# Hybrid decoder layer on one core: the recurrence without GpSimd arithmetic, with a shifted decay and v copied across halves

## The chip, the core and the metric

One core of a Trainium2 chip runs the whole layer. TensorE (PE) multiplies, with its weight loads shown apart as PEld; VectorE (DVE) and ScalarE (ACT) work element by element; GpSimd (POOL) does some arithmetic, memsets and DMA issue; SyncE (SP) issues the weight DMAs. The metric is the device time of one execution in microseconds; less is better. Each engine takes its instructions in the order in which the program has them.

## The reference

A decoder layer for 256 tokens of width 2048: RMSNorm, one input projection (6432 columns), then two groups side by side, 16 dilated-attention heads and 16 RWKV-7 heads, an output projection with residual, and a SwiGLU feed-forward of 5632 with residual and a last norm. The part around the change is the RWKV-7 group:

```python
decay = jnp.exp(-DECAY_SCALE * jax.nn.sigmoid(w0 + jnp.tanh(w_lo) @ w_up))
a = jax.nn.sigmoid(a0 + a_lo @ a_up)
kk = heads(k * k_k)
kk = kk / jnp.maximum(jnp.sqrt(jnp.sum(kk * kk, axis=-1, keepdims=True)), 1e-12)
k = k * (1.0 + (a - 1.0) * k_a)
xs = (rh, wh, kh, vh, -kk, kk * ah)          # by token
def rwkv7_step(state, inp):
    r, w, k, v, a, bb = inp
    sa = jnp.einsum('bhij,bhj->bhi', state, a)
    state = (state * w[:, :, None, :] + sa[..., None] * bb[:, :, None, :]
             + v[..., None] * k[:, :, None, :])
    y = jnp.einsum('bhij,bhj->bhi', state, r)
    return state, y
```

## The kernel before

All large products run in fp32r pieces: a weight tile `wr` that SP loads is split by ACT into `wh` (L148) and by DVE into the rest `wl` (L149, one 128x512 instruction), and PE multiplies three times (for the projections in transposed form L191 to L193, 128x256 each; for v and the later products L178 to L180). So every half weight tile costs DVE one L149, and twelve projection matmuls eat it up. PE's main stream of projections goes through the kernel from end to end.

The recurrence and the attention are side threads: Python generators whose steps are mixed into the main stream by a virtual clock (`run`, `step`; a `yield 2.0` asks for a pause of so much), so the order on each engine is fixed when the program is built. The RWKV heads come in two halves of 8 heads (`half` 0 and 1). A half works on tiles of 4 x 256 columns (4 pairs of heads, 256 tokens) in these stages:

- `keys` (L513 on): `tha` is the tanh of the a gate, `kp` the changed key, `kn` the key at unit length, with `blocksum` for sums over 64 rows;
- `core`: `thp` and its scan `sc` (L552) are the logarithm of the decay, summed over 64 tokens; `pw` (L557) and `ipw` (L559) are the decay from the chunk's start and its inverse, inclusive of the token, `pm` (L561) the exclusive one; `ar` holds per chunk of 64 tokens the key side (index 0, L572) and the receptance side (index 1, L586); `bk` holds the products with `ipw` (L580, L582);
- 64x64 products `Ah` (L616), and the inverse of a triangular matrix by 31 steps on DVE (`T1`, L655 and L657, from `nu`, which a DMA brings); `T1` and its transpose go to DRAM (L673, L676) and come back by quarters as `T` and `U64` (L688, L689, issued on ACT's queue) for the products `C0` and `C1`; then the chunk loop (`Xh`, `Yh`, `Zh`, `Hh`);
- `end`: two `blocksum` of y (L783), two of its squares `sq` (L787), the gate product `gh` (16 matmuls, L796) and the last factors (L789 to L800). The `end` of half 0 stands amid the `core` of half 1.

`blocksum` (L478 on) cuts a tile into halves of 512 columns; for each, ACT writes `bh` (L483), DVE the rest `bl` (L484), and PE adds L487 (with `bh`) and L488 (with `bl`) in its order. v is put into a tile `vs` with the two 64-token halves exchanged (L596, GpSimd), transposed on PE (L640) and copied by ACT (L642) into `vv`.

Of the kernel before, what the change touches and what calls it, by code (L numbers as in the profile page):

```python
# [10 lines left out]
F32 = mybir.dt.float32  # L11
F32R = mybir.dt.float32r
AF = mybir.ActivationFunctionType
ALU = mybir.AluOpType
AX = mybir.AxisListType

P = 128
SEQ = 256
D = 2048
HD = 64  # L20
# [10 lines left out]
DS = math.exp(-0.5)  # L31
# [44 lines left out]
def layer(ctx: ExitStack, tc: tile.TileContext, I, out, dbg=None, upto=99):  # L76
# [344 lines left out]
    for dst, c0, n, i in ((wa, 0, 128, 0), (gl0, 128, 128, 1), (gl1, 256, 32, 2)):  # L421
        pt = opsum(f"ptlo{i}")
# [38 lines left out]
    def rwkv_side(half, hb, H, e, Z):  # L461
# [46 lines left out]
        def ln_table(ins):  # L508

            with tc.issue_after(getattr(ins, "ins", ins)):  # L510
                ACT.preload_act_table_set("natural_log_exp_and_others")

        def keys():  # L513

            tha = e(7, "tha") if half == 0 else e(3, "tha")
            yield from up(tha, lo_up()[64:128, :], wa[64:128, :], AF.Tanh, 8, "a")
            if half == 1:
                ln_table(Z["tanh"])
            zk = yield from need("zk")

            kp = e(8, "kp") if half == 0 else e(10, "kp")
            for hp in range(4):
                b = hb + hp
                DVE.tensor_scalar(kp[:, hp, :], tha[:, hp, :], hv[:, 16 + b:17 + b], hv[:, 24 + b:25 + b],
                                  op0=ALU.mult, op1=ALU.add)
            yield 2.0
            POOL.tensor_tensor(fl(kp), fl(kp), fl(zk), op=ALU.mult)

            kn = (e(9, "kn") if half == 0 else
                  act_p.tile([P, 4, SEQ], F32, tag="mx0", name=f"kn_{H}"))  # L530
            for hp in range(4):
                ACT.activation(kn[:, hp, :], zk[:, hp, :], AF.Square, scale=hpc(V_KK, hp))
            yield from blocksum(kn, lambda pt, sl: DVE.tensor_scalar(fl(kn)[:, sl], pt, 1e-24, None, op0=ALU.max))
            ACT.activation(fl(kn), fl(kn), AF.Ln)
            yield 2.0
            ACT.activation(fl(kn), fl(kn), AF.Exp, scale=-0.5)
            yield 2.0
            for hp in range(4):
                DVE.scalar_tensor_tensor(kn[:, hp, :], zk[:, hp, :], hpc(V_KK, hp), kn[:, hp, :],
                                         op0=ALU.mult, op1=ALU.mult)  # L540
            yield EL
            DVE.scalar_tensor_tensor(fl(tha), fl(tha), 1.0, fl(kn), op0=ALU.add, op1=ALU.mult)
            Z["tha"], Z["kp"], Z["kn"] = tha, kp, kn

        def core():
# [6 lines left out]
                DVE.tensor_tensor_scan(sc[:, hp, :], packc(C_SCAN, SEQ), thp[:, hp, :], 0.0,  # L552
                                       op0=ALU.mult, op1=ALU.add)
            yield 2.0
            POOL.tensor_tensor(fl(thp), fl(sc), fl(thp), op=ALU.subtract)
            pw = e(6, "pw")
            ACT.activation(fl(pw), fl(sc), AF.Exp, scale=-0.5 * DS)  # L557
            yield 2.0
            ACT.activation(fl(sc), fl(sc), AF.Exp, scale=0.5 * DS)  # L559
            yield 2.0  # L560
            ln_table(ACT.activation(fl(thp), fl(thp), AF.Exp, scale=-0.5 * DS))  # L561
            ipw, pm = sc, thp
            pcs = rp.tile([P, 4, 4], F32, tag="pcs", name=f"pcs{H}")
            DVE.tensor_copy(pcs, pw[:, :, HD - 1::HD])

# [3 lines left out]

            ar = rp.tile([P, 4, 4, 2, HD], F32, tag="ar", name=f"ar{H}")  # L570
            yield EL
            DVE.scalar_tensor_tensor(ar[:, :, :, 0, :], ch(kn), -1.0, ch(pm), op0=ALU.mult, op1=ALU.mult)  # L572
            yield EL

            bk = [e(i, f"bk{i}").rearrange("p a (c w t) -> p (a c) w t", w=2, t=HD) for i in (4, 2)]
# [1 line left out]
            for g in range(2):  # L577
                for c2 in range(2):
                    pr = lambda a: ch(a)[:, 2 * g:2 * g + 2, c2::2, :]
                    DVE.scalar_tensor_tensor(bk[g][:, :, c2::2, c2, :], pr(tha), 0.5, pr(ipw),  # L580
                                             op0=ALU.mult, op1=ALU.mult)
                    POOL.tensor_tensor(bk[g][:, :, c2::2, 1 - c2, :], pr(ipw), pr(kp), op=ALU.mult)  # L582
                yield EL

            zr = yield from need("zr")
            POOL.tensor_tensor(ar[:, :, :, 1, :], ch(zr), ch(pw), op=ALU.mult)  # L586
            yield EL
            for hp in range(4):
                DVE.scalar_tensor_tensor(kp[:, hp, :], zr[:, hp, :], hpc(V_RK, hp), kp[:, hp, :],
# [1 line left out]
            zv = yield from need("zv")  # L591
            yield from blocksum(kp, lambda pt, sl: DVE.tensor_tensor(fl(kp)[:, sl], pt, fl(zv)[:, sl], op=ALU.mult))
            bonus = kp
            vs = rp.tile([P, 4, 2, P], F32, tag="e9", name=f"vs{H}")
            for c2 in range(2):
                POOL.tensor_copy(vs[:, :, :, 64 * (1 - c2):64 * (1 - c2) + 64], ch(zv)[:, :, c2::2, :])  # L596

# [23 lines left out]
                    q = 2 * c2 + b  # L623
                    ACT.dma_start(block(d1, q)[:, 8 * cp:8 * cp + 8, :], abk[quarter(q), c, :, 32 * b:32 * b + 32])
            flat = lambda t: t.rearrange("p a b -> p (a b)")[0:HD].rearrange("p (s t) -> p s t", t=32)
            T1 = flat(e(3, "T1"))
            POOL.memset(T1, 0.0)
            POOL.memset(T1.rearrange("p a b -> p (a b)")[:, 0::33], 1.0)

            vv = [e(i, f"vv{i}").rearrange("p (c a) (b i) -> p c (a b) i", c=2, i=HD) for i in (5, 7)]  # L630
            for c in range(4):
# [5 lines left out]
            for cp in range(2):  # L637
                pt = opsum(f"tv{H}{cp}")
                for hp in range(4):
                    PE.transpose(pt[:, hp * P:(hp + 1) * P], vs[:, hp, cp], ident)  # L640
                for c2 in range(2):
                    ACT.copy(vv[cp][half_of(1 - c2), c2, :, :], pt[half_of(1 - c2)].rearrange("p (h j) -> p h j", j=HD))  # L642
                if cp == 0:
                    nu = flat(e(6, "nu"))
                    ACT.dma_start(nu, d1.rearrange("u (s t) -> u s t", t=32))
                yield
            yield LAT[0]


# [469 lines left out]
```

## Time and profile before

| | us |
|---|---|
| median of 3 runs | 1251.55 (1250.91 to 1253.92) |
| the profiled execution's own time | 1252.15 |
| its span, first to last instruction | 1250.2 |
| PE busy in the span | 1227.6 (98%) |
| DVE busy | 815.4 (65%) |
| ACT busy | 692.9 (55%) |
| POOL busy | 63.7 (5%) |

The span is what the views divide; the execution's own time has 1.95 us more around it. A busy PE in this table only says that some matmul was under way; time that it lost shows as idle time before an instruction, with the instruction that ended it, and as a granted clock below 1.

### The profile page before, as it was taken

The page shows a single profiled execution, that of the slowest core. Times are in us where ns is not written, and L with a number is a line of the kernel's source. Part 1 is how long each engine was busy: PE and PEld are TensorE (multiplying, and loading weights), DVE is VectorE, ACT ScalarE, POOL GpSimd, SP SyncE. Part 2 cuts the span into 40 slices and gives each one's busy share as a digit, 9 for nine tenths or more (in the row PEclk, how much of TensorE's full clock was granted, in tenths as well). Part 3 has the DMA queues.
Part 4 walks back from the last instruction along what each step waited for, and adds up shares of the span by engine and source line. Part 5 has one row for each costly group of instructions (what it writes and reads, how often), then busy time and mean ns, then how long its engine had stood idle before and what let it go on. Part 6 is the DMA issues. An engine that isn't in the chain of part 4 may idle for free.

```text
span 1250.2 us, 21170 instructions
## 1 busy us (share of the span) xinstructions
PE 1227.6 (98%) x7930; PEld 1065.7 (85%) x7930; DVE 815.4 (65%) x1519; ACT 692.9 (55%) x1312; POOL 63.7 (5%) x69
## 2 busy tenths in 40 slices
PE   7999999999999999999999999999999999999997
PEld 6999997888899788888888888888888888888885
DVE  5787885587946857665665666666566565555653
ACT  7755655555645756565555655555565554454443
POOL 3140000120000000000000000000000000010100
PEclk9999999999999999999999999999999999999999
DMA  8657575335563476666666666666666666666664
GB/s 236 185 151 199 153 193 139 111 113 135 157 178 106 145 226 215 180 186 190 187 191 194 187 188 193 192 187 186 197 189 187 191 193 187 195 188 193 183 201 134
DMA packets 147879, 223.24 MB, mean 179 GB/s; under 512 B 18123, under 2 KB 65489, under 8 KB 147649
## 3 DMA queue, kind: packets, MB, share of 16 engines
q1 hardware_dynamic: 132176, 211.12, 57.7%
q10 hardware_dynamic: 13920, 6.06, 2.0%
q0 software_dynamic: 1680, 4.72, 1.1%
q8 instruction: 62, 1.02, 0.3%
q14 instruction: 41, 0.33, 0.1%
HBM read 218.17 MB, written 3.69 MB: 177 GB/s over the span
## 4 chain that ended last, share of the span: by engine, by line
PE 90%; DVE 4%; DMA 3%; ACT 1%; issue 1%; SPq 0%; POOLq 0%; POOL 0%; ACTq 0%; DVEq 0%
PE up L1000 13%; PE gb L1000 7%; PE ga L1000 7%; PE up L1001 6%; PE d L178 6%; PE d L180 6%; PE d L179 6%; PE gb L1001 3%; PE ga L1001 3%; DMA wr<-in_w_in_dram 2%; PE o L179 2%; PE o L180 2%; PE o L178 2%; PE qTb L191 1%; PE zrh L191 1%; PE qTb L192 1%
## 5 line engine op out<-in xcount | busy, mean ns | idle before, releaser
L149 DVE TENSOR_TENSOR wl<-wr,wh 128x512 fp32r<-128x512 f32 (+1 forms) x792 | 549.6, 700 | 367.6 <-ACT wh L148 350.9
L148 ACT ACTIVATE wh<-wr 128x512 fp32r<-128x512 f32 (+1 forms) x792 | 492.1, 627 | 470.7 <-DVE wl L149 202.1
L1000 PE MATMUL up<-u,wh 128*128 128x512 f32 x704 | 244.6, 394 | 0.0
L1001 PE MATMUL up<-u,wl 128*128 128x256 f32 x704 | 195.0, 277 | 0.0
L1000 PEld LDWEIGHTS up<-u,wh 128*128 128x128 f32 x704 | 132.0, 188 | 30.6
L1001 PEld LDWEIGHTS up<-u,wl 128*128 128x128 f32 x704 | 132.2, 188 | 0.0
L178 PE MATMUL d<-wh,hh 128*128 128x512 f32 x336 | 131.5, 391 | 0.0
L179 PE MATMUL d<-wl,hh 128*128 128x512 f32 x336 | 131.5, 391 | 0.0
L180 PE MATMUL d<-wh,hl 128*128 128x512 f32 x336 | 131.5, 391 | 0.0
L1000 PE MATMUL gb<-u,wh 128*128 128x512 f32 x352 | 130.4, 394 | 0.0
L1000 PE MATMUL ga<-u,wh 128*128 128x512 f32 x352 | 130.1, 394 | 0.0
L1001 PE MATMUL gb<-u,wl 128*128 128x256 f32 x352 | 97.6, 277 | 0.0
L1001 PE MATMUL ga<-u,wl 128*128 128x256 f32 x352 | 97.6, 277 | 0.0
L1000 PEld LDWEIGHTS ga<-u,wh 128*128 128x128 f32 x352 | 66.0, 188 | 15.3
L1000 PEld LDWEIGHTS gb<-u,wh 128*128 128x128 f32 x352 | 66.0, 188 | 15.3
L180 PEld LDWEIGHTS d<-wh,hl 128*128 128x128 f32 x336 | 63.2, 188 | 13.8
L179 PEld LDWEIGHTS d<-wl,hh 128*128 128x128 f32 x336 | 63.2, 188 | 13.8
L178 PEld LDWEIGHTS d<-wh,hh 128*128 128x128 f32 x336 | 63.2, 188 | 13.8
L1001 PEld LDWEIGHTS gb<-u,wl 128*128 128x128 f32 x352 | 66.2, 188 | 0.0
L1001 PEld LDWEIGHTS ga<-u,wl 128*128 128x128 f32 x352 | 66.0, 188 | 0.1
L1053 POOL TENSOR_TENSOR h_sb<-h_sb,fg 128x512 f32<-128x512 f32 x6 | 9.9, 1659 | 663.0 <-ACT jd L1051 663.0
L191 PE MATMUL kTb<-u1h,wh 128*128 128x256 f32 x128 | 38.1, 298 | 0.0
(293 smaller groups left out, 2095.6 us busy)
## 6 DMA issues: line engine op xcount, KB each, us to landing
wr<-in_w_gate_up_dram SPq DMA_DIRECT2D x176, 512.0 KB, 4.3
wr<-in_w_in_dram SPq DMA_DIRECT2D x96, 512.0 KB, 3.8
wr<-in_w_down_dram SPq DMA_DIRECT2D x88, 512.0 KB, 4.5
wr<-in_w_out_dram SPq DMA_DIRECT2D x32, 512.0 KB, 4.7
wr<-in_w_in_dram SPq DMA_DIRECT2D x8, 288.0 KB, 6.1
x_sb<-in_x_dram SPq DMA_DIRECT2D x8, 256.0 KB, 6.6
biasa<-rvd ACTq DMA_DIRECT2D x4, 512.0 KB, 4.7
xs<-in_x_dram POOLq DMA_DIRECT2D x4, 512.0 KB, 6.4
```

What stands on the lines that cost most here:

```text
L148: ACT.activation(hi[:, :, :n], src, AF.Copy)
L149: DVE.tensor_tensor(lo[:, :, :n], src, hi[:, :, :n].bitcast(F32), op=ALU.subtract)
L178: PE.matmul(o, ah[:, sl], hi[:, :n], start=first, stop=False)
L179: PE.matmul(o, ah[:, sl], lo[:, :n], start=False, stop=False)
L180: PE.matmul(o, al[:, sl], hi[:, :n], start=False, stop=fin)
L191: PE.matmul(o, hi[:, cb], uh_, start=kc == 0, stop=False)
L192: PE.matmul(o, hi[:, cb], ul_, start=False, stop=False)
L1000: PE.matmul(ps[b], hi[:, cb], u, start=kc == 0, stop=False)
L1001: PE.matmul(ps[b][:, 0:SEQ], lo[:, cb], u[:, 0, :], start=False, stop=kc == NK - 1)
L1053: POOL.tensor_tensor(hs, hs, fg[:, cs], op=ALU.mult)
```

## The change

In words: five operations go from GpSimd to DVE, namely `kp` times `zk` (L527, one 128x1024 instruction in each half), the four products of `bk` (L582; in the new file L583) and `zr` times `pw` (L586, now four instructions, L588). The exclusive decay `pm` is not made any more: GpSimd's subtraction (L555) and ACT's third exponential (L561) go, and the key side of `ar` takes `pw` of the token before (four instructions of 63 columns, and one for each chunk's first token, where the exclusive decay is 1; L570 and L572 of the new file). The exchanged copy `vs` (L596) goes; v is transposed as it is, and ACT's copy moves the result across the two halves of the partitions. The two memsets of `T1` stay on GpSimd but stand behind the transposes of v.

```diff
             yield 2.0
-            POOL.tensor_tensor(fl(kp), fl(kp), fl(zk), op=ALU.mult)
+            DVE.tensor_tensor(fl(kp), fl(kp), fl(zk), op=ALU.mult)
...
-            POOL.tensor_tensor(fl(thp), fl(sc), fl(thp), op=ALU.subtract)
             pw = e(6, "pw")
             ACT.activation(fl(pw), fl(sc), AF.Exp, scale=-0.5 * DS)
             yield 2.0
-            ACT.activation(fl(sc), fl(sc), AF.Exp, scale=0.5 * DS)
-            yield 2.0
-            ln_table(ACT.activation(fl(thp), fl(thp), AF.Exp, scale=-0.5 * DS))
-            ipw, pm = sc, thp
+            ln_table(ACT.activation(fl(sc), fl(sc), AF.Exp, scale=0.5 * DS))
+            ipw = sc
...
-            DVE.scalar_tensor_tensor(ar[:, :, :, 0, :], ch(kn), -1.0, ch(pm), op0=ALU.mult, op1=ALU.mult)
+            DVE.tensor_scalar(ar[:, :, :, 0, 0:1], ch(kn)[:, :, :, 0:1], -1.0, None, op0=ALU.mult)
+            for hp in range(4):
+                DVE.scalar_tensor_tensor(ar[:, hp, :, 0, 1:HD], ch(kn)[:, hp, :, 1:HD], -1.0,
+                                         ch(pw)[:, hp, :, 0:HD - 1], op0=ALU.mult, op1=ALU.mult)
...
-                    POOL.tensor_tensor(bk[g][:, :, c2::2, 1 - c2, :], pr(ipw), pr(kp), op=ALU.mult)
+                    DVE.tensor_tensor(bk[g][:, :, c2::2, 1 - c2, :], pr(ipw), pr(kp), op=ALU.mult)
...
-            POOL.tensor_tensor(ar[:, :, :, 1, :], ch(zr), ch(pw), op=ALU.mult)
+            for hp in range(4):
+                DVE.tensor_tensor(ar[:, hp, :, 1, :], ch(zr)[:, hp], ch(pw)[:, hp], op=ALU.mult)
...
-            vs = rp.tile([P, 4, 2, P], F32, tag="e9", name=f"vs{H}")
-            for c2 in range(2):
-                POOL.tensor_copy(vs[:, :, :, 64 * (1 - c2):64 * (1 - c2) + 64], ch(zv)[:, :, c2::2, :])
...
-            T1 = flat(e(3, "T1"))
-            POOL.memset(T1, 0.0)
-            POOL.memset(T1.rearrange("p a b -> p (a b)")[:, 0::33], 1.0)
...
-                    PE.transpose(pt[:, hp * P:(hp + 1) * P], vs[:, hp, cp], ident)
+                    PE.transpose(pt[:, hp * P:(hp + 1) * P], zv[:, hp, cp * P:(cp + 1) * P], ident)
                 for c2 in range(2):
-                    ACT.copy(vv[cp][half_of(1 - c2), c2, :, :], pt[half_of(1 - c2)].rearrange("p (h j) -> p h j", j=HD))
+                    ACT.copy(vv[cp][half_of(1 - c2), c2, :, :], pt[half_of(c2)].rearrange("p (h j) -> p h j", j=HD))
...
+            T1 = flat(e(3, "T1"))
+            POOL.memset(T1, 0.0)
+            POOL.memset(T1.rearrange("p a b -> p (a b)")[:, 0::33], 1.0)
             yield LAT[0]
```

The pauses of the threads shift with it, and so does the order on each engine. Three places matter. The first is DVE where the `end` of half 0 and the `core` of half 1 meet, from the second `blh` of y (L484) to the first `blh` of its squares; before:

```order
L484 TENSOR_TENSOR blh0_3256<-y_h0_2801,bhh0_3255 128x512
L149 TENSOR_TENSOR wl71_0_3242<-wr71_3239,wh71_0_3241 128x512
L783 SCALAR_TENSOR_TENSOR y_h0_2801<-bsh0_3272,y_h0_2801 128x512
L149 TENSOR_TENSOR wl71_1_3246<-wr71_3239,wh71_1_3245 128x512
L564 COPY pcsh1_3278<-pw_h1_3227 128x16
L572 SCALAR_TENSOR_TENSOR arh1_3280<-kn_h1_2727,thp_h1_3151 128x16x64
L580 SCALAR_TENSOR_TENSOR bk4_h1_3326<-tha_h1_2633,sc_h1_3197 128x4x64 x2
L149 TENSOR_TENSOR wl72_0_3290<-wr72_3287,wh72_0_3289 128x512
L149 TENSOR_TENSOR wl72_1_3294<-wr72_3287,wh72_1_3293 128x512
L589 SCALAR_TENSOR_TENSOR kp_h1_2670<-zr_h1_1885,par_76,kp_h1_2670 128x256 x2
L149 TENSOR_TENSOR wl73_0_3341<-wr73_3338,wh73_0_3340 128x512
L484 TENSOR_TENSOR blh0_3306<-sq_h0_3303,bhh0_3305 128x512
```

The same stretch of DVE in the changed kernel:

```order
L484 TENSOR_TENSOR blh0_3257<-y_h0_2803,bhh0_3256 128x512
L149 TENSOR_TENSOR wl71_0_3243<-wr71_3240,wh71_0_3242 128x512
L561 COPY pcsh1_3262<-pw_h1_3228 128x16
L783 SCALAR_TENSOR_TENSOR y_h0_2803<-bsh0_3277,y_h0_2803 128x512
L149 TENSOR_TENSOR wl71_1_3247<-wr71_3240,wh71_1_3246 128x512
L572 SCALAR_TENSOR_TENSOR arh1_3264<-kn_h1_2729,pw_h1_3228 128x4x63 x4
L149 TENSOR_TENSOR wl72_0_3295<-wr72_3292,wh72_0_3294 128x512
L581 SCALAR_TENSOR_TENSOR bk4_h1_3314<-tha_h1_2635,sc_h1_3199 128x4x64
L583 TENSOR_TENSOR bk4_h1_3314<-sc_h1_3199,kp_h1_2672 128x4x64
L149 TENSOR_TENSOR wl72_1_3299<-wr72_3292,wh72_1_3298 128x512
L484 TENSOR_TENSOR blh0_3311<-sq_h0_3308,bhh0_3310 128x512
```

One weight piece (`wl73_0`) and two `kp` products now come behind the last row; one former GpSimd product (L583) and the `ar` in four pieces stand ahead of it. Between the two `blh` of `sq` DVE now has three 128x256 and 128x512 rows (L581, L583, `wl73_0`).

The second place is the next stretch of DVE in the changed kernel, from the second `blh` of `sq` to the first `blh` of half 1's `kp`:

```order
L484 TENSOR_TENSOR blh0_3363<-sq_h0_3308,bhh0_3362 128x512
L149 TENSOR_TENSOR wl73_1_3353<-wr73_3346,wh73_1_3352 128x512
L588 TENSOR_TENSOR arh1_3264<-zr_h1_1884,pw_h1_3228 128x4x64 x4
L591 SCALAR_TENSOR_TENSOR kp_h1_2672<-zr_h1_1884,par_76,kp_h1_2672 128x256 x2
L149 TENSOR_TENSOR wl74_0_3403<-wr74_3400,wh74_0_3402 128x512
L789 TENSOR_TENSOR y_h0_2803<-y_h0_2803,sq_h0_3308 128x1024
L484 TENSOR_TENSOR blh1_3391<-kp_h1_2672,bhh1_3390 128x512
```

Before, one `wl` alone stood between these two `blh`, and L789 behind them.

The third is PE at the second attention quad of the first head half: before, the products `AVh10` of half 1's recurrence came behind its transposes `PTa1`:

```order
L868 MATMUL PTa10_3989<-ident_72,sa1_3941 128x128 x2
L868 MATMUL PTa11_3995<-ident_72,sa1_3941 128x128 x3
L667 MATMUL AVh10_4001<-vv5_h1_3686,abkh1_3552 64x64 x16
L875 MATMUL Oa10_4019<-pTa10_3990,vb0_2986 64x256
L875 MATMUL Oa10_4019<-pTa11_3996,vb0_2986 64x256
```

In the changed kernel they stand right behind the scores `Sa1`:

```order
L842 MATMUL Sa110_3964<-kTb0_3459,qTb0_2991 128x256
L842 MATMUL Sa111_3965<-kTb0_3459,qTb0_2991 128x256
L667 MATMUL AVh10_3974<-vv5_h1_3661,abkh1_3534 64x64 x16
L179 MATMUL vb1_1_4066<-wl83_0_4076,u1h1_89 128x512
L180 MATMUL vb1_1_4066<-wh83_0_4075,u1l1_93 128x512
```

From `Sa1` to the first `PTa1` PE then has 25 matmuls of the main stream and the `AVh10`, where before it had 32 of the main stream. Elsewhere PE's order is nearly the old one; the second half's products come 12 projection matmuls earlier.

## Rows read from the trace of the kernel before

**Rows 1.** The page, busy time of each engine in us (share), number of instructions.

```profile
PE 1227.6 (98%) x7930; PEld 1065.7 (85%) x7930; DVE 815.4 (65%) x1519; ACT 692.9 (55%) x1312; POOL 63.7 (5%) x69
```

**Rows 2.** Waits of PE: line, who ended them, us in total, times, longest.

```profile
PE bsh L488 <- DVE blh L484: 5.0, 3, 2.8
```

**Rows 3.** Windows of 10 us: busy us of PE, PEld, DVE, ACT, POOL; clock, DMA.

```profile
80.00:90.00 10.00, 10.00 (x86) 10.00 (x85) 10.00 (x13) 4.47 (x8) 10.00 (x5) 1.00 0.61 172
...
250.00:260.00 10.00, 7.51 (x58) 7.14 (x58) 9.97 (x13) 6.86 (x10) 3.98 (x3) 1.00 0.24 60
260.00:270.00 10.00, 9.70 (x45) 7.68 (x46) 6.87 (x13) 4.62 (x7) 3.21 (x5) 0.83 0.43 133
```

**Rows 4.** Timeline of PE: start, us, instruction, count, [idle before, ended by].

```profile
112.97 0.51 PE L488 MATMUL bsh<-blh,onesblk 128*128 128x512 f32 x1 [0.65 <-DVE blh L484]
...
248.08 0.28 PE L192 MATMUL qTb<-u1l,wh 128*128 128x256 f32 x1
249.96 0.51 PE L488 MATMUL bsh<-blh,onesblk 128*128 128x512 f32 x1 [1.60 <-DVE blh L484]
...
257.11 0.28 PE L193 MATMUL qTb<-u1h,wl 128*128 128x256 f32 x1
257.23 0.28 PE L191 MATMUL qTb<-u1h,wh 128*128 128x256 f32 x1
260.30 0.50 PE L488 MATMUL bsh<-blh,onesblk 128*128 128x512 f32 x1 [2.79 <-DVE blh L484]
```

**Rows 5.** Timeline of DVE ahead of these waits.

```profile
111.26 1.05 DVE L149 TENSOR_TENSOR wl<-wr,wh 128x512 fp32r<-128x512 f32 x1
...
247.47 0.75 DVE L822 TENSOR_TENSOR qTb<-qTb,rbc 128x256 f32<-128x256 f32 x2
248.13 1.77 DVE L484 TENSOR_TENSOR blh<-y_h,bhh 128x512 fp32r<-128x512 f32 x1
249.82 2.89 DVE L149 TENSOR_TENSOR wl<-wr,wh 128x512 fp32r<-128x512 f32 x1
...
255.17 1.32 DVE L580 SCALAR_TENSOR_TENSOR bk_h<-tha_h,sc_h 128x256 f32<-128x256 f32 x2
256.41 1.83 DVE L149 TENSOR_TENSOR wl<-wr,wh 128x512 fp32r<-128x512 f32 x2
...
259.56 0.68 DVE L484 TENSOR_TENSOR blh<-sq_h,bhh 128x512 fp32r<-128x512 f32 x1
```

**Rows 6.** Timeline of POOL in the same stretch.

```profile
246.97 2.38 POOL L555 TENSOR_TENSOR thp_h<-sc_h,thp_h 128x1024 f32<-128x1024 f32 x1 [4.58 <-DVE sc_h L552]
249.31 2.85 POOL L586 TENSOR_TENSOR arh<-zr_h,pw_h 128x1024 f32<-128x1024 f32 x1
255.28 1.81 POOL L582 TENSOR_TENSOR bk_h<-sc_h,kp_h 128x256 f32<-128x256 f32 x2 [3.12 <-DVE arh L572]
```

**Rows 7.** Groups by form, 30 to 440 us: count, busy us, mean ns, idle before.

```profile
L580 DVE SCALAR_TENSOR_TENSOR bk_h<-tha_h,sc_h 128x256 f32<-128x256 f32 x8 | 5.8, 764 | 0.1
L572 DVE SCALAR_TENSOR_TENSOR arh<-kn_h,thp_h 128x1024 f32<-128x1024 f32 x2 | 2.4, 1220 | 0.0
L755 DVE TENSOR_TENSOR Sh<-Sh,pcsh 128x256 f32<-128x256 f32 x4 | 1.7, 423 | 0.1
L642 ACT COPY vv_h<-tvh 64x512 f32<-64x512 f32 x8 | 4.7, 582 | 0.1
L675 ACT COPY U_h<-T_h 64x1024 f32<-64x1024 f32 x2 | 4.2, 2087 | 0.4 <-issue 0.4
```

**Rows 8.** The chain that ended last: the second half's gate product; start, us.

```profile
408.11 3.84 PE gh L796 x16
```

**Rows 9.** Timeline of PE at the second attention quad.

```profile
325.48 0.33 PE L868 MATMUL PTa<-ident,sa 128*128 128x128 f32 x1
```

**Rows 10.** Timelines: ACT's last issues of the first half's inverse, and PE's `C0`.

```profile
192.62 0.85 ACTq L689 DMA_DIRECT2D U_h<-d2h  x2
...
199.07 1.20 PE L699 MATMUL C0h<-T_h,abkh 32*32 32x32 f32 x64
```

**Rows 11.** DMA issues: queue, count, KB each, median us from issue to landing.

```profile
T_h<-d2h ACTq DMA_DIRECT2D x4, 64.0 KB, 4.6
```

## The prediction

> **What bounds the kernel now.** I read the page first: PE is busy 1227.6 of 1250.2 us, DVE 815.4, POOL only 63.7 [rows 1]. So the kernel ends when PE's stream ends, and a change beside PE is worth only what PE waits or loses clock for it; PE's own work stays the same here. The next view is therefore PE's waits. From 30 us on, one line stands out: L488 of `blocksum` waited for DVE's `blh` (L484) 5.0 us in three places, the longest 2.8 us [rows 2]. The windows show what lies around them: from 250 to 260 us PE is busy 7.51 us of 10 and DVE 9.97, and in the next ten the granted clock is 0.83 [rows 3]. A window at 0.83 between the chip's levels of 2.4 and 1.2 GHz means about 3.4 us at the lower one, behind PE's idle time, so 1.7 us of work is lost there.
>
> Then I asked for the timelines at the three waits. By starts, where the matmul before leads to the next after 0.12 us (257.11 to 257.23), the wait at 248.08 cost 249.96 - 248.08 - 0.12 = 1.76 us and that at 257.23 cost 3.07 - 0.12 = 2.95 us; the early one is 0.65 us of idle time [rows 4]. DVE's timeline says why `blh` came late: a 128x512 instruction takes 0.68 us (259.56), but `blh` at 248.13 took 1.77 us and the `wl` behind it 2.89 [rows 5]. At these times GpSimd ran L555 (246.97 to 249.35) and L586 (249.31 to 252.16) [rows 6]. Both DVE instructions read two SBUF tensors, and both end some 0.55 us after the GpSimd instruction does (249.90 and 252.71), about their own time. The two `qTb` products at 247.47, with one input in PSUM, ran beside L555 at 0.75 us for both [rows 5]. So here a GpSimd instruction that reads SBUF holds up DVE's instructions with two SBUF inputs until it is through.
>
> **The change, part by part.** I sum against the profiled execution (1252.15 us) and carry the difference over to the median (1251.55 us), which lies 0.6 us lower.
>
> *What DVE loses.* The two blocked instructions give back 1.77 - 0.68 = 1.09 and 2.89 - 0.68 = 2.21 us. The pair of L580 at 255.17 took 1.32 us and the two `wl` at 256.41 took 1.83, each some 0.5 us too long beside L582 [rows 5, 6], 1.0 us together; the `wl` at 111.26 was 0.37 too long. That is 4.7 us, and the first half has more of it, which no PE wait shows.
>
> *What DVE gains.* In each half one 128x1024 product at 1.22 us and eight of 128x256 (four L583, four L588) at 0.42 [rows 7]; four pieces of `ar` at 0.42 and one small one instead of one at 1.22, so 0.6 more. Together 1.22 + 3.4 + 0.6 = 5.2 us a half. Nearly all is cover: DVE's sum hardly changes, but the blocked time stood ahead of `blh`, and the new work mostly does not.
>
> *The wait at 112.97.* The `wl` ahead of `blh` loses its 0.37: gain 0.35 us.
>
> *The wait at 249.96.* PE's order here is unchanged and `blh` ends 1.09 us earlier: gain 1.1 of the 1.76; the rest is DVE's own queue of scans and stays.
>
> *The wait at 260.30.* From the end of the y `blh` to the end of the first `sq` `blh`, the changed order has five 128x512 rows, six of 128x256 and a small copy: 5 x 0.68 + 6 x 0.42 + 0.2 = 6.1 us at full durations, some 5.5 with the 0.07 us by which DVE's instructions overlap. PE covers it with two `blocksum` matmuls and 44 projection matmuls at 0.12, 5.7 us. Before, DVE needed 249.90 to 260.24, 10.3 us. I take 2.8 of the 2.95 us as gained.
>
> *The clock.* With the two long waits gone I take it that PE does not fall to the lower level; gain 1.6 of the 1.7 us. If the rest of the waits is still enough for it, 0.
>
> *New waits.* (a) The second `sq` `blh` now has L581, L583 and a `wl` ahead: 0.42 + 0.42 + 0.68 + 0.68 = 2.2 us against 11 projection matmuls and one of `blocksum` on PE, 1.55: I take 0.3 us lost (0 to 0.7). (b) The `kp` `blh` behind it has 2 x 0.68 for `wl`, 6 x 0.42, L789 at 1.22 and its own 0.68: 5.8 us at full durations, 5.2 overlapped. PE covers with `gh`, 3.84 us where it ran at full clock [rows 8], nine projection matmuls and L487: 5.15. I take 0 (up to 0.7). (c) At the second attention quad the first `PTa1` started at 325.48 when DVE had its input ready [rows 9]. PE now reaches it with 25 instead of 32 main matmuls and the `AVh10` ahead, some 0.5 us sooner, and DVE's order there is the old one: 0.5 us lost.
>
> *Costed at nothing.* ACT's copy across halves is not in the trace; nearest are the copy within a half (582 ns) and the strided `U_h` copy, 2087 ns for twice the columns [rows 7], so 0 to 0.46 us more for each of eight. ACT does not bound there, and the `AVh` that need them come much later: 0. ACT loses two exponentials, off the path: 0. GpSimd's later memset delays the first DVE step on `T1`; see rival two.
>
> Sum: 0.35 + 1.1 + 2.8 + 1.6 - 0.3 - 0.5 = 5.05, so 5.0 us. The profiled execution would be 1247.1, the median **1246.5 us**. Everything behind 440 us is the same PE-bound stream, so the gain arrives in full.
>
> **The rivals.** *One: DVE becomes the bound.* It is full already from 80 to 90 us and nearly so from 250 to 260 [rows 3], and gets 5.2 us a half of its own. Were the new 128x256 products as slow as L580's mean of 764 ns [rows 7], the seven or so that stand between the `blh` above would cost 7 x 0.34 = 2.4 us, nearly all on PE, and the gain would be 2.6: 1249 us, within no change. Against it: L580's mean contains the blocking that goes; the free ones took 0.42. The Trainium skill (Perfetto Trace Analysis, Optimizing Scalar/DVE Operations) names moving work off a saturated DVE, even to GpSimd, as an option, which would speak against this change; it adds that the two share an SBUF read port, so that it might not help, and the rows here side with the second half of that advice.
>
> *Two, slower: the inverse comes too late.* In the first half `T1` is now cleared only behind the transposes of v, and its chain of 31 steps ends four `wl` later, 4 x 12 x 0.12 = 5.8 us. Its reads back were issued until 193.47 and took 4.6 us to land, 198.1, against PE's `C0` at 199.07, in the same PE place after the change [rows 10, 11]: 1 us of slack. In the changed ACT order four reads stand at that end where two stood, in a gap of ACT. If instead the chain's 5.8 us went through, PE would stand for 4.8 us, lose 1.6 to the clock again, and for the same in half 1 another 6.4: 1246.5 + 12.8 = 1259 us. It decides from a loss of 8.8 us on. For it: PE takes `C0` in order and cannot go around. Against it: before, the reads waited for their place on ACT's queue rather than for data.
>
> *Three: it isn't GpSimd.* If the long DVE instructions have another cause, only the new waits stay: 1251.55 + 0.8 = 1252.3, no change. The matching ends above speak strongly against it.
>
> **How the numbers follow.** Forecast 0.68, rival one 0.18, two 0.08, three 0.06. A measurement tells about 0.3%, 3.8 us, from no change, so faster means under 1247.8. The forecast's own spread comes from the bounds: all waits and the clock regained is 0.8 + 1.8 + 2.9 + 1.7 = 7.2, so 1244.4; with the clock lost, 1248.1. Faster gets 0.64 of the forecast's chance and 0.02 of rival one's: 0.66; same 0.04 + 0.16 + 0.06 = 0.26; slower 0.08. The range runs from 1244.4 to 1250.4, leaving out rivals two and three and a little at either end.
>
> **What would show it.** Right: no DVE 128x512 instruction over 0.8 us between 30 and 440 us; PE's waits for `blh` under 2 us in all; a clock of 1.00 around 260 us; POOL busy under 40 us. Wrong: a wait of PE at L699 or L702 for ACT or a DMA (rival two), DVE at ten tenths ahead of a waiting L488 (rival one), or the 0.83 still there. Above all a new wait over 2 us anywhere before 440 us would refute the sum.

## The result, and the profile of the changed kernel

The changed kernel took 1245.48 us (median of its runs) against 1251.55 before, a ratio of 0.9950 with a 95% interval of 0.9938 to 0.9963: 0.5% faster, which is small but more than the 0.3% that a measurement can tell. One of its five executions took 3096.3 us; it counts in that median, not in the ratio. Forecast were 1246.5 us, within 1244.4 to 1250.4, and 0.66 for faster. A second comparison, with a second profile of each kernel (`ctl_after` below), gave 0.9939 (0.9925 to 0.9952). The profiled execution took 1245.13 us with a span of 1243.1, before 1252.15 and 1250.2.

The page first: busy time and instructions of each engine.

```profile
PE 1226.2 (99%) x7930; PEld 1065.7 (86%) x7930; DVE 811.9 (65%) x1545; ACT 693.5 (56%) x1310; POOL 33.0 (3%) x51
```

Against [rows 1] GpSimd lost 31 us of its 64 and 18 instructions, nine in each half: the six products that went to DVE (one L527, four L582, one L586), the subtraction L555 and the two copies of v. And yet DVE, which took over the work, is no busier: 811.9 us with 26 instructions more, where it was 815.4. Either this is less work than it looks, or the old sum held time in which DVE stood. PE's waits (us in total, times, longest) show where the kernel felt it:

```profile
PE PTa L868 <- DVE sa L860: 1.5, 2, 1.3
...
PE bsh L488 <- DVE blh L484: 0.5, 1, 0.5
```

The 5.0 us in three places of [rows 2] are 0.5 in one. The largest wait behind the kernel's start is now another one, that of the first attention quad's transposes for the softmax; it was there before, with 1.01 us. The windows that answer to [rows 3] (busy us of PE, PEld, DVE, ACT, POOL, then clock, DMA share and GB/s):

```profile
80.00:90.00 10.00, 10.00 (x86) 10.00 (x85) 10.00 (x26) 5.23 (x9) 0.00 (x0) 1.00 0.70 202
...
250.00:260.00 10.00, 10.00 (x66) 8.64 (x64) 9.85 (x21) 7.92 (x13) 0.55 (x1) 1.00 0.58 161
260.00:270.00 10.00, 10.00 (x82) 9.12 (x81) 10.00 (x24) 3.68 (x6) 1.62 (x3) 1.00 0.29 84
```

Read the first row for DVE: ten tenths busy before and after, but 26 instructions now pass through where 13 did. Part of this is smaller pieces (`ar` comes in four), part is time in which the old ones stood: three L580 at 87.78 us took 3.30 us together in the kernel before, three of the same four products (now L581, at 85.50 us) take 1.09. A busy share does not tell work from standing. In 250 to 260 us PE went from 7.51 to 10.00, at a granted clock of 1.00 throughout. PE's L488 there, for y, for the squares and for `kp`, where [rows 4] had 1.60 and 2.79 us of idle time at the first two:

```profile
247.81 0.50 PE L488 MATMUL bsh<-blh,onesblk 128*128 128x512 f32 x1 [0.45 <-DVE blh L484]
...
253.89 0.40 PE L488 MATMUL bsh<-blh,onesblk 128*128 128x512 f32 x1
...
261.04 0.40 PE L488 MATMUL bsh<-blh,onesblk 128*128 128x512 f32 x1
```

DVE's own timeline of that stretch (start, us, instruction):

```profile
247.08 0.68 DVE L484 TENSOR_TENSOR blh<-y_h,bhh 128x512 fp32r<-128x512 f32 x1
247.68 0.68 DVE L149 TENSOR_TENSOR wl<-wr,wh 128x512 fp32r<-128x512 f32 x1
...
252.91 0.69 DVE L484 TENSOR_TENSOR blh<-sq_h,bhh 128x512 fp32r<-128x512 f32 x1
253.51 0.42 DVE L581 SCALAR_TENSOR_TENSOR bk_h<-tha_h,sc_h 128x256 f32<-128x256 f32 x1
253.85 0.42 DVE L583 TENSOR_TENSOR bk_h<-sc_h,kp_h 128x256 f32<-128x256 f32 x1
...
260.05 0.68 DVE L484 TENSOR_TENSOR blh<-kp_h,bhh 128x512 fp32r<-128x512 f32 x1
```

The `blh` of y took 0.68 us instead of 1.77, the `wl` behind it 0.68 instead of 2.89 [rows 5]. From the end of that `blh` (247.76) to the end of the first `sq` `blh` (253.60) are 5.8 us; before, 10.3. The groups of the new products (count | busy us, mean ns):

```profile
L583 DVE TENSOR_TENSOR bk_h<-sc_h,kp_h 128x256 f32<-128x256 f32 x8 | 3.3, 418 | 0.0
L581 DVE SCALAR_TENSOR_TENSOR bk_h<-tha_h,sc_h 128x256 f32<-128x256 f32 x8 | 3.2, 417 | 0.0
L588 DVE TENSOR_TENSOR arh<-zr_h,pw_h 128x256 f32<-128x256 f32 x8 | 3.0, 417 | 0.0
L572 DVE SCALAR_TENSOR_TENSOR arh<-kn_h,pw_h 128x252 f32<-128x252 f32 x8 | 2.9, 414 | 0.0
L527 DVE TENSOR_TENSOR kp_h<-kp_h,zk_h 128x1024 f32<-128x1024 f32 x2 | 2.4, 1222 | 0.0
```

L581 is the old L580 unchanged: 764 ns before [rows 7], 417 now. And ACT's copy across halves costs what the copy within one did, 582 ns:

```profile
L639 ACT COPY vv_h<-tvh 64x512 f32<-64x512 f32 x8 | 4.6, 581 | 0.1
```

**Where the time came from.** The start of the program is the same code in both, but the first `up_wh` came at 35.40 us before and at 34.72 after, and between 33.7 and 35.9 in the thirteen profiles of this study. So I compare a stretch that leaves it out, from the first `up_wh` to the feed-forward's first matmul, by PE's timeline:

```profile
34.72 1.99 PE L469 MATMUL up_wh<-wa,lo_up 64*128 64x256 f32 x8
...
502.20 0.39 PE L1000 MATMUL ga<-u,wh 128*128 128x512 f32 x1
```

That is 467.48 us, before 509.43 - 35.40 = 474.03: 6.55 us less. What follows it is alike (1243.1 - 502.20 = 740.9 and 740.8 us). Below this stretch is called the **core stretch**. It is finer than the medians, which carry the start, but it is one execution per number: the two profiles of the kernel before differ by 1.45 us in it, those of the changed kernel by 0.32.

| kernel | median us | ratio to before (95%) | core stretch us |
|---|---|---|---|
| before, first and second profile | 1251.55 | | 474.03, 472.58 |
| changed, first and second profile | 1245.48 | 0.9950 (0.9938 to 0.9963) | 467.48, 467.16 |
| `p_v` | 1251.88 | 1.0001 (0.9989 to 1.0014) | 474.52 |
| `p_shift` | 1249.17 | 0.9979 (0.9969 to 0.9988) | 471.34 |
| `p_products` | 1246.06 | 0.9950 (0.9934 to 0.9966) | 468.57 |
| `ab_only` | 1244.08 | 0.9943 (0.9931 to 0.9956) | 466.81 |
| `d_two` | 1247.24 | 0.9964 (0.9951 to 0.9978) | 469.38 |
| `d_one` | 1246.46 | 0.9963 (0.9950 to 0.9975) | 468.80 |
| `d_none` | 1243.90 | 0.9943 (0.9930 to 0.9955) | 467.17 |
| `d_load` | 1246.79 | 0.9957 (0.9943 to 0.9972) | 468.65 |
| `i_pause` | 1246.43 | 0.9961 (0.9949 to 0.9974) | 468.83 |

### The profile page after: what moved, and what is told of

It reads as the page before. It is cut to its first block, busy times and chain, and to the rows that moved or that the text cites. A ratio compares the mean times of both kernels' runs of the same rounds, so it can differ in the third digit from the quotient of the medians.

```text
span 1243.1 us, 21171 instructions
## 1 busy us (share of the span) xinstructions
PE 1226.2 (99%) x7930; PEld 1065.7 (86%) x7930; DVE 811.9 (65%) x1545; ACT 693.5 (56%) x1310; POOL 33.0 (3%) x51
## 4 chain that ended last, share of the span: by engine, by line
PE 94%; DMA 2%; DVE 2%; ACT 1%; issue 1%; SPq 0%; POOLq 0%; POOL 0%; ACTq 0%; DVEq 0%
PE up L1000 13%; PE gb L1000 7%; PE ga L1000 7%; PE up L1001 7%; PE d L180 6%; PE d L179 6%; PE d L178 6%; PE gb L1001 3%; PE ga L1001 3%; DMA wr<-in_w_in_dram 2%; PE o L179 2%; PE o L180 2%; PE o L178 2%; PE kTb L191 1%; PE qTb L191 1%; PE zkh L191 1%
## 5 line engine op out<-in xcount | busy, mean ns | idle before, releaser
L149 DVE TENSOR_TENSOR wl<-wr,wh 128x512 fp32r<-128x512 f32 (+1 forms) x792 | 542.8, 691 | 359.4 <-ACT wh L148 342.0
L178 PE MATMUL o<-wh,mixh 128*128 128x512 f32 x96 | 37.5, 391 | 0.0
```

The lines of the kernel that those rows point to most:

```text
L149: DVE.tensor_tensor(lo[:, :, :n], src, hi[:, :, :n].bitcast(F32), op=ALU.subtract)
L178: PE.matmul(o, ah[:, sl], hi[:, :n], start=first, stop=False)
```

## Experiments

The theory: GpSimd's instructions that read SBUF held up DVE's instructions with two SBUF inputs, and through `blh` PE; the change gains because they are gone. The rivals: the gain is one of order (fewer pauses, other places), or of less work. Two sets of kernels: the change cut into its parts, and the changed kernel with idle GpSimd work put back.

### The parts: v alone (`p_v`)

```
-  vs = rp.tile(...); POOL.tensor_copy(vs..., zv...)   # twice
-  PE.transpose(..., vs[:, hp, cp], ident)
+  PE.transpose(..., zv[:, hp, cp * P:(cp + 1) * P], ident)
-  ACT.copy(vv[cp][half_of(1 - c2), ...], pt[half_of(1 - c2)]...)
+  ACT.copy(vv[cp][half_of(1 - c2), ...], pt[half_of(c2)]...)
```
T1's two memsets move behind it, as in the change.

> The kernel before with the part on v alone: v transposed as it is, the two GpSimd copies gone, ACT's copies across halves, T1 cleared later. Contention theory: only the copy at 110.21 us of [rows 6] had stood beside a DVE instruction ahead of a waiting L488, so the wait at 112.97 us falls from 0.65 us of idle time to 0.3 or less and the time by 0.4 to 0.9 us, to about 1251.0 by the median; the waits at 249.96 and 260.30 and the 0.83 clock stay. Rival (the gain comes from v, since fewer copies shorten the way to A): the long waits shrink too, 1247. Rival two of the prediction (T1 too late): a wait at C0, 1259.

Measured: ratio 1.0001. The long waits stand as before, and with them the lower clock (0.94 and 0.72 in the two windows of ten us from 250):

```profile
249.21 0.50 PE L488 MATMUL bsh<-blh,onesblk 128*128 128x512 f32 x1 [1.55 <-DVE blh L484]
...
259.54 0.79 PE L488 MATMUL bsh<-blh,onesblk 128*128 128x512 f32 x1 [2.77 <-DVE blh L484]
```

The wait at 112.97 us is gone, as expected (what that is worth: see `ctl_before`); the 0.4 to 0.9 us that this was to bring do not show in the time. PE waited at no `C0`, so rival two of the prediction is out. The part on v brings nothing that can be measured.

### The parts: the shifted decay alone (`p_shift`)

```
-  POOL.tensor_tensor(fl(thp), fl(sc), fl(thp), op=ALU.subtract)
-  ACT.activation(fl(sc), ...); yield 2.0
-  ln_table(ACT.activation(fl(thp), ...))
+  ln_table(ACT.activation(fl(sc), ...))
-  DVE.scalar_tensor_tensor(ar[:, :, :, 0, :], ch(kn), -1.0, ch(pm), ...)
+  DVE.tensor_scalar(ar[:, :, :, 0, 0:1], ...)
+  for hp in range(4): DVE.scalar_tensor_tensor(ar[:, hp, :, 0, 1:HD], ..., ch(pw)[:, hp, :, 0:HD - 1], ...)
```

> The kernel before with the decay shifted by a token and its subtraction L555 gone, all products still on GpSimd. Contention theory: GpSimd's zr*pw no longer stands behind L555, so it starts when pw is there, about 247.9 us, runs 2.85 us and now holds the y blh itself: that ends near 251.3 instead of 249.90, the y wait grows from 1.76 to about 3 us, the wl behind it comes free (0.7 us), and the sq wait shrinks to about 1 us; the clock is still lost; 1250 to 1251.5. Rival (what delayed blh was DVE's own queue and the order of the work, not GpSimd): the y wait does not grow.

This run sets the theory against the rivals most sharply, since it foretells that taking a GpSimd instruction away makes a wait longer. GpSimd, DVE and PE there:

```profile
246.59 2.34 POOL L586 TENSOR_TENSOR arh<-zr_h,pw_h 128x1024 f32<-128x1024 f32 x1 [5.63 <-ACT pw_h L556]
248.91 2.33 POOL L582 TENSOR_TENSOR bk_h<-sc_h,kp_h 128x256 f32<-128x256 f32 x2
```

```profile
246.71 2.78 DVE L484 TENSOR_TENSOR blh<-y_h,bhh 128x512 fp32r<-128x512 f32 x1
249.41 1.22 DVE L149 TENSOR_TENSOR wl<-wr,wh 128x512 fp32r<-128x512 f32 x1
```

```profile
249.54 0.50 PE L488 MATMUL bsh<-blh,onesblk 128*128 128x512 f32 x1 [2.61 <-DVE blh L484]
...
256.32 0.50 PE L488 MATMUL bsh<-blh,onesblk 128*128 128x512 f32 x1 [0.77 <-DVE blh L484]
```

zr*pw started 0.12 us ahead of `blh` (at 246.59, sooner than the expected 247.9) and `blh` then took 2.78 us, to 0.56 behind zr*pw's end. The y wait grew from 1.60 to 2.61 us of idle time, the sq wait fell to 0.77: both as expected. Two misses: the clock stayed at 1.00 in the windows from 250 to 270 us, and the time, 1249.17 us, came out below the expected 1250.

### The parts: the products alone (`p_products`)

```
-  POOL.tensor_tensor(fl(kp), fl(kp), fl(zk), op=ALU.mult)
+  DVE.tensor_tensor(fl(kp), fl(kp), fl(zk), op=ALU.mult)
-  POOL.tensor_tensor(bk[g]..., pr(ipw), pr(kp), op=ALU.mult)
+  DVE.tensor_tensor(bk[g]..., pr(ipw), pr(kp), op=ALU.mult)
-  POOL.tensor_tensor(ar[:, :, :, 1, :], ch(zr), ch(pw), op=ALU.mult)
+  for hp in range(4): DVE.tensor_tensor(ar[:, hp, :, 1, :], ch(zr)[:, hp], ch(pw)[:, hp], op=ALU.mult)
```

> The kernel before with the products L527, L582 and L586 on DVE (L586 in four pieces), the subtraction L555 and the v copies still on GpSimd. Contention theory: the y wait stays at about 1.7 us (L555 still holds blh), the wait at 112.97 stays, the wl behind is free, and from the end of the y blh to the end of the first sq blh DVE needs about 7.5 us instead of 10.3, so the sq wait falls from 2.95 to about 0.1 to 0.5 and the clock comes back or not: 1246.5 to 1249.5, most likely 1247.5. Rival (DVE becomes the bound by its own new work): the sq wait stays near 3 us, 1251 or more.

GpSimd, DVE and PE there:

```profile
244.49 2.37 POOL L555 TENSOR_TENSOR thp_h<-sc_h,thp_h 128x1024 f32<-128x1024 f32 x1 [4.69 <-DVE sc_h L552]
```

```profile
245.56 1.84 DVE L484 TENSOR_TENSOR blh<-y_h,bhh 128x512 fp32r<-128x512 f32 x1
247.33 0.68 DVE L149 TENSOR_TENSOR wl<-wr,wh 128x512 fp32r<-128x512 f32 x1
```

```profile
247.46 0.50 PE L488 MATMUL bsh<-blh,onesblk 128*128 128x512 f32 x1 [1.67 <-DVE blh L484]
...
255.09 0.40 PE L488 MATMUL bsh<-blh,onesblk 128*128 128x512 f32 x1
```

The y wait stayed: L555 still reads, and `blh` took 1.84 us, to 0.54 behind L555's end, while the `wl` behind it was free. The sq wait went altogether, the clock was 1.00, and the ratio is that of the whole change, 0.9950; in the core stretch it is 1.1 us behind it, as the y wait that stayed leads one to expect. DVE's extra work did not bind: against rival one. Two misses: the wait at 112.97 did not stay, and the time, 1246.06 us, lies below the expected 1246.5 to 1249.5.

### Products and decay, without v (`ab_only`)

The changed kernel with the lines of `p_v` turned back:

```
+  vs = rp.tile(...); POOL.tensor_copy(vs..., zv...)   # twice
-  PE.transpose(..., zv[:, hp, cp * P:(cp + 1) * P], ident)
+  PE.transpose(..., vs[:, hp, cp], ident)
-  ACT.copy(vv[cp][half_of(1 - c2), ...], pt[half_of(c2)]...)
+  ACT.copy(vv[cp][half_of(1 - c2), ...], pt[half_of(1 - c2)]...)
```

> The changed kernel with v as it was before (two GpSimd copies into vs, ACT's copies within a half, T1 cleared early); products and decay as in the change. If products and decay carry the gain and the part on v adds nothing lasting, the y wait is about 0.5 us, the sq wait gone, the clock 1.00, and the time that of the changed kernel, 1245.5 within 1. If the copies of v on GpSimd cost by themselves, a DVE instruction of 128x512 over 0.8 us stands beside them and a wait at L488 of 0.3 to 0.9 us in the first half comes back.

Measured 0.9943, the core stretch 466.81 us against 467.48 and 467.16; the y wait 0.51 us, the sq wait none. The time, 1244.08 us, is below the expected 1244.5 to 1246.5, but next to the changed kernel's 1244.30 in the same comparison. The part on v can be left out. The two GpSimd copies into `vs` do no harm here: they run from 106.52 to 108.18 us, the one `wl` beside them had started 0.06 us ahead and kept 0.69 us, and the next starts at 108.37, behind them.

### Idle GpSimd work put back: two reads, one read, none (`d_two`, `d_one`, `d_none`)

In the changed kernel `thp` is dead behind the scans of the second half. Three kernels put work on it there, for which nobody waits until much later; the order on PE, DVE and ACT is that of the changed kernel, instruction for instruction.

```
   yield 2.0
+  if half == 1:
+      for _ in range(2): POOL.tensor_tensor(fl(thp), fl(thp), fl(thp), op=ALU.add)   # d_two
+      for _ in range(3): POOL.tensor_copy(fl(thp), fl(thp))                          # d_one
+      for _ in range(5): POOL.memset(fl(thp), 0.0)                                   # d_none
   pw = e(6, "pw")
```

> The changed kernel with two GpSimd additions of thp to itself (two SBUF reads, 128x1024, nobody waits for them before bk) put into the second half behind the scans, where L555 and L586 stood before. Contention theory: they run 2.4 us each from about 246 to 251 us; the DVE instruction with two SBUF inputs that meets each one is held until about 0.55 us behind its end: L484 for y takes about 1.8 us or more and a wl about 2.4 to 2.9, the y wait grows from 0.45 to about 2 us and the sq wait comes back at about 2 us: 3 to 5.3 us slower than the changed kernel with the clock, 1248.5 to 1251. Rival (order and dependencies made the waits, GpSimd's reads don't matter): 1245.5.

> The same place, three GpSimd copies of thp onto itself instead (one SBUF read each, 128x1024, about 1.56 us each by the copies of v at half the columns twice over). If one read is enough to hold DVE (the wl at 111.26 us was 0.37 us long beside the copy of v), some three DVE instructions are held for up to 1 us each and it is 1 to 4 us slower than the changed kernel; if it takes two reads, 1245.5.

> The same place, five GpSimd memsets of thp instead (no SBUF read, about 1 us each, 5 us in all). Contention by reads: DVE's instructions keep 0.69 us and the time is the changed kernel's, 1245.5 within 0.5. Rival (any GpSimd instruction that writes SBUF holds DVE): as slow as the two additions, 1248.5 to 1251.

GpSimd and then DVE, in `d_two`, `d_one` and `d_none`, each from its own timeline:

```profile
246.82 4.19 POOL L557 TENSOR_TENSOR thp_h<-thp_h 128x1024 f32<-128x1024 f32 x2 [4.54 <-DVE sc_h L552]
...
247.32 0.75 DVE L825 TENSOR_TENSOR qTb<-qTb,rbc 128x256 f32<-128x256 f32 x2
247.98 1.27 DVE L484 TENSOR_TENSOR blh<-y_h,bhh 128x512 fp32r<-128x512 f32 x1
249.18 2.38 DVE L149 TENSOR_TENSOR wl<-wr,wh 128x512 fp32r<-128x512 f32 x1
```

```profile
247.11 3.58 POOL L557 COPY thp_h<-thp_h 128x1024 f32<-128x1024 f32 x3 [4.55 <-DVE sc_h L552]
...
248.27 1.52 DVE L484 TENSOR_TENSOR blh<-y_h,bhh 128x512 fp32r<-128x512 f32 x1
249.72 1.52 DVE L149 TENSOR_TENSOR wl<-wr,wh 128x512 fp32r<-128x512 f32 x1
```

```profile
245.56 5.01 POOL L557 MEMSET thp_h<- 128x1024 f32 x5 [4.52 <-DVE sc_h L552]
...
246.75 0.68 DVE L484 TENSOR_TENSOR blh<-y_h,bhh 128x512 fp32r<-128x512 f32 x1
247.35 0.69 DVE L149 TENSOR_TENSOR wl<-wr,wh 128x512 fp32r<-128x512 f32 x1
```

The same DVE instructions at the same place: 1.27 and 2.38 us beside two reads, 1.52 and 1.52 beside one, 0.68 and 0.69 beside memsets, though these kept GpSimd busy longest. The pair L825, with one input in PSUM, ran at 0.75 beside the additions too. PE followed: it waited 1.04 and 1.06 us at L488 in `d_two`, 1.29 and 0.53 in `d_one`, and 0.45 in `d_none`, exactly as in the changed kernel. In the core stretch the reads cost 1.9 and 1.3 us, the memsets -0.3. With one order for all, the rival of order is out, and since 5 us more of memsets cost nothing, the amount of GpSimd's work is not it either. My sizes were too large: the additions took 1.89 and 2.22 us, not 2.4 each, the copies 1.04 to 1.38, not 1.56, the waits in `d_two` stayed at half of the 2 us expected, and the clock stayed at 1.00, so 1247.24 instead of 1248.5 or more. `d_none` at 1243.90 us lies below the expected 1245.0 to 1246.0; the changed kernel itself took 1244.30 in its second comparison.

The Trainium skill (SBUF — State Buffer, Who interferes with whom) says that a DVE instruction with two SBUF inputs contends with a GpSimd instruction that reads SBUF, but not with one that only writes it; these three runs agree, with 2.38, 1.52 and 0.69 us for the `wl`.

### More work on DVE (`d_load`)

```
-  for hp in range(4):
+  for hp in list(range(4)) * (3 if half else 1):
       DVE.tensor_tensor(ar[:, hp, :, 1, :], ch(zr)[:, hp], ch(pw)[:, hp], op=ALU.mult)
```

> The changed kernel with the four products zr*pw of the second half (L588) done three times over on DVE: 8 x 0.34 = 2.7 us more of DVE between the second sq blh and the first kp blh. If DVE stands at its edge there (the kp blh ended at 260.73 and L488 started at 261.04, 0.3 us of slack), PE waits 2.4 us more at L488, with the clock up to 4 us: 1248 to 1249.5. If DVE has room there that the wait did not show (rival), 1245.5.

The twelve products took 4.11 us at 255.26, and yet PE did not wait at L488. I had left out that PE's order is made anew when the program is built: it now has L488 of the first `kp` further back, at 262.77 us, 0.27 behind the end of `blh` at 262.50, where the changed kernel had 0.31. The cost came elsewhere: the core stretch is 1.2 us longer than in the changed kernel. From one PE start to the next, the matmuls of `Ah` took 2.1 us more (11.0 against 8.9 us); in the second half one of their four groups of 16 is split in two there. The wait at the first attention quad fell from 1.26 to 0.69 us against it. Why `Ah` is slower in that order is not shown. So the expected time was nearly right (1246.8 against 1248 or more) and its mechanism wrong. Whether DVE is at its edge there is not settled by this run; that the order took up 2.7 us of it is.

### A pause ahead of the attention's transposes (`i_pause`)

```
+  yield 2.0
   for hp in range(2):
       pTs = []
```

> The changed kernel with a pause of 2.0 on the schedule's clock between the softmax and the transposes of each attention quad, so that PE's main stream stands ahead of the first PTa, where the changed kernel still waits 1.26 us for sa (and 0.26 at the fourth quad). Theory: those waits go and nothing is late behind them: 1244.0. Rival: the pause moves the next steps of the side work onto other places, and a new wait takes back as much or more: 1245.5 to 1247.

The rival came true: the wait fell from 1.26 to 0.92 only and that of 0.26 at the fourth quad went, but one of 0.21 arose at the second quad and, in the second half's chain, one of 1.00 us at L738, for which the profile names no releaser; 1246.43 us.

### Controls: both kernels once more (`ctl_before`, `ctl_after`)

> The kernel before once more, for a second profile. The waits at 249.96 (1.6 us idle) and 260.30 (2.8) and the half clock behind them come from the order and from GpSimd and are there again within 0.2 us. The first matmul of up_wh, at 35.40 us in the first profile, moves by up to 1 us with the loads at the start. Whether the wait at 112.97 (0.65) is there again is open: ACT's wh ahead of it had waited for a DMA.

> The changed kernel once more, for a second profile and a second comparison: the ratio to the kernel before within 0.9938 to 0.9963, no wait over 0.6 us between up_wh and the first attention quad, 1.2 us there, and a start that moves by up to 1 us against the first profile (34.72 for up_wh).

The second profile of the changed kernel is like the first (0.45 us at y, 1.16 at the first quad). The second of the kernel before is not, in two places. Its two long waits are there to 0.04 us, but the lower clock behind them is not, and the wait at 112.97 is missing:

```profile
248.67 0.50 PE L488 MATMUL bsh<-blh,onesblk 128*128 128x512 f32 x1 [1.60 <-DVE blh L484]
...
259.00 0.50 PE L488 MATMUL bsh<-blh,onesblk 128*128 128x512 f32 x1 [2.75 <-DVE blh L484]
```

```profile
260.00:270.00 10.00, 10.00 (x65) 8.68 (x65) 8.68 (x14) 4.81 (x8) 3.67 (x6) 1.00 0.35 94
```

For the missing one, first GpSimd's copy of v in the first profile of the kernel before, the one that the expectation of `p_v` means (it is not among [rows 6]):

```profile
110.21 1.56 POOL L596 COPY vsh<-zv_h 128x512 f32<-128x512 f32 x2 [20.09 <-DVE zv_h L414]
```

Then ACT's timeline a few us earlier, in the first profile of the kernel before and in the second:

```profile
106.73 1.15 ACT L148 ACTIVATE wh<-wr 128x512 fp32r<-128x512 f32 x2 [2.62 <-DMA wr<-in_w_in_dram]
```

```profile
105.43 1.15 ACT L148 ACTIVATE wh<-wr 128x512 fp32r<-128x512 f32 x2 [1.77 <-DMA wr<-in_w_in_dram]
```

The `wl` beside the copy of v was long in both (1.05 and 1.06 us), and a weight tile had come late in both, but ACT waited 0.85 us longer for it in the first. From the start of L487 to that of the matmul behind L488 PE took 0.93 us more than in the changed kernel in the first profile (111.92 to 113.31 against 111.24 to 111.70) and 0.29 in the second (111.26 to 112.01); in `p_v`, where ACT had waited 1.72 us at that place and no copy stood beside the `wl`, it took no more. So what I read as one wait in the first profile had two causes: some 0.3 us by the copy, and another 0.64 that came only with that run's later tile.

## Why the prediction was right

By its own steps, against the first pair of profiles:

| term | forecast us | measured us |
|---|---|---|
| wait at 112.97 | 0.35 | 0.93 |
| wait at 249.96 | 1.1 | 1.76 - 0.61 = 1.15 |
| wait at 260.30 | 2.8 | 2.95 |
| clock | 1.6 | 1.7 |
| second `sq` `blh` (a), `kp` `blh` (b) | -0.3, 0 | 0, 0 |
| second attention quad (c) | -0.5 | +0.07 |
| first attention quad | not seen | -0.25 |
| sum | 5.05 | 6.55 |

The measured terms add up to the 6.55 us of the core stretch. That they do so to the last digit is partly chance: summed by tile, from one PE start to the next, smaller shifts stand against each other, `Oa` 0.37, `PTa` 0.28 and `Ah` 0.21 us shorter, `Xh` 0.28, `Sa` 0.12 and `qTb` outside its two waits 0.4 longer. (0.61 is the y wait by starts: 247.81 - 247.08 - 0.12, as the prediction counts; 0.93 is explained at `ctl_before`; 1.7 is the window of 0.83 against 1.00.)

**The cause** was named rightly: the ends that matched in [rows 5, 6] were no chance, as `p_shift` and the three runs with idle GpSimd work show. **What DVE gains**: 0.42 us a product was right, to 5 ns. **The waits at 249.96 and 260.30** came out within 0.15 us, and `p_shift` and `p_products` show which GpSimd instruction stood behind which. At 260.30 two errors of the working met, and the result is partly luck. From the y `blh` to the first `sq` `blh` the changed order has six 128x512 rows, not five (four `wl`, L783, `blh`): 6.8 us at full durations, and DVE took 5.84. PE's cover was 6.08 us (247.81 to 253.89), not 5.7, since each of the two `blocksum` matmuls held the next start back by 0.34 us. Six rows against 5.7 us would have left some 0.3 us of wait by the working's own overlap, an estimate; none came.

**Mis-sized were the small terms.** The wait at 112.97 went entirely, where I gave only the 0.37 us of the held `wl`; the other 0.58 came with a late weight transfer of that run (0.64 by `ctl_before`), which the row ahead (ACT's wait for the DMA) would have told. And the new waits, 0.8 us in my sum, did not come. For (a) I set 2.2 us of DVE against 1.55 of PE; measured from `blh` to `blh` (253.60 to 255.47) and from L488 to L488 (253.89 to 255.66) they were 1.87 and 1.77, since DVE's instructions overlap and two `blocksum` matmuls, not one, lie between the two starts; and `blh` had come 0.29 us early. For (b) they were 5.26 and 5.38, where I had 5.2 and 5.15. (c) did not show at all, and why is not shown; the first quad lost 0.25 instead, which the sum had not looked at. By the rows of the table 0.58 + 0.05 + 0.15 + 0.10 + 0.30 + 0.57 - 0.25 = 1.50 us is what the sum was too low.

**The clock** was rightly sized. `ctl_before` has the order of the kernel before and no lower clock there: from L488 for the squares to the second part of `gh` PE took 4.78 us in the first profile (260.30 to 265.08) and 3.18 in the second (259.00 to 262.18), 1.6 us less for the same matmuls. Six of them, before and in `ctl_before`:

```profile
262.42 2.73 PE L796 MATMUL gh<-gl,g_up0h 128*128 128x256 f32 x6
```

```profile
260.79 1.46 PE L796 MATMUL gh<-gl,g_up0h 128*128 128x256 f32 x6
```

It is still the term to be careful with: after the same two waits the lower level came in two of three profiles (before and `p_v` yes, `ctl_before` no). By the second pair of profiles, without it and without most of the wait at 112.97, the change is worth 472.58 - 467.16 = 5.4 us, of which 1.0 is a wait for ACT's `bhh` that only that profile of before has. That pair is the low end, though. The profiled execution `ctl_before` took 1249.63 us at a mean granted clock of 0.999; the nine timed executions of the kernel before in that comparison took 1250.38 to 1253.38 us at 0.995 to 0.997, and the medians lie 7.6 us apart (1251.94 and 1244.30). Where those executions lost their time is not on record.

**Rivals.** One (DVE becomes the bound) fell: in `p_products` DVE has all the products and PE no wait behind y's. The Trainium skill (Perfetto Trace Analysis, Optimizing Scalar/DVE Operations) says that moving work off a saturated DVE, even to GpSimd, may make sense, and adds that the two share an SBUF read port, so that it might not help; the traces agree with the second half, since the DVE that read ten tenths from 80 to 90 us was in part standing (3.30 us for three L580 that now take 1.09). Two (the inverse too late) fell: no wait of PE at L699 or L702 in the changed kernel, nor in `p_v`. Three (not GpSimd) fell by `d_two` against `d_none`.

**What would show it** held in each point. The one line for all `wl` from 30 to 440 us (minimum, median and maximum in ns, first and last start), before and then after:

```profile
L149 DVE TENSOR_TENSOR wl<-wr,wh x209: 666/685/2900, 29.3 to 439.3; 128x512 fp32r<-128x512 f32 x105
```

```profile
L149 DVE TENSOR_TENSOR wl<-wr,wh x213: 666/686/695, 30.4 to 439.7; 128x512 fp32r<-128x512 f32 x107
```

The medians are alike; only the long ones are gone. Then 0.5 us of `blh` waits, clock 1.00 around 260 us, POOL 33.0 us, no new wait over 2 us.

## What to carry to other kernels

Where a saturated DVE shares a stretch with GpSimd, look at the means of one and the same form: instructions with two SBUF inputs that take 0.68 us in one place and 1.8 to 2.9 in another, ending just behind a GpSimd instruction, are standing, and giving DVE that GpSimd work can cost it nothing. Memsets may stay on GpSimd as far as such instructions go, and so may reads that meet none of them ahead of a wait of the bounding engine. Before a term is booked, ask whether a second execution would show it: waits that end at a DMA and the lower clock may not come again.

## What I had not expected of the hardware

One read is enough. A GpSimd copy with a single SBUF input held DVE as the two-input addition did: 1.52 us for a 0.68 us instruction. And the hold goes both ways: GpSimd's zr*pw took 2.85 us in the kernel before [rows 6], where the held `blh` ran through its first 0.6 us, and 2.34 in `p_shift`, where it had started ahead of DVE's `blh`. In `d_two` the first addition took 1.89 us and the second, beside the released `blh`, 2.22; in `d_one` the three copies took 1.04, 1.04 and, beside the released `blh`, 1.38.

A memset is not harmless to every DVE instruction. `pcsh`, a copy of 128x16 with one SBUF input, took 0.62 us beside a memset in `d_none` and 0.71 beside L582 in `p_shift`, and 0.16 to 0.18 in the other 24 places of the thirteen profiles. No wait of PE followed from it, and no run was made for it.

The lower clock does not follow from the waits alone. PE idled 1.60 and 2.75 us around 249 and 259 us in `ctl_before` and 1.55 and 2.77 in `p_v`, with clocks of 1.00 and 0.72 in the ten us from 260. What else decides was not tried.

The Trainium skill (TensorE: Matmul & The Clock Gate, What's actually happening) says that the gate's window runs freely, so that one and the same kernel can differ from run to run; it says so of a kernel's start. The pair of profiles of the kernel before differs in the middle of the kernel, 0.83 [rows 3] and 1.00, which fits, but no run shows that the window is the reason.
